# The second down-projection as seven block products, with sums made by accumulating transfers

## The chip, the cores and the metric

The kernel runs on one core of a Trainium2 chip. The metric is the device time in microseconds of one execution, as the median of several runs. TensorE (PE) multiplies, VectorE (DVE) and ScalarE (ACT) work on tiles, GpSimd (POOL) does a little of both and has a DMA queue of its own, and SyncE (SP) issues most of the transfers. Each engine takes its instructions strictly in the order in which they stand in its queue.

## The reference

Two decoder layers over 1024 tokens of 1024 channels, in float32. The first layer mixes by a short convolution and by attention, the second by the RWKV recurrence. Each is followed by the same channel mixer, and the change concerns this one, above all in the second layer:

```python
D_MODEL, SEQ, D_FF = 1024, 1024, 2816

def conv_glu_ffn(x, w_up, conv_w, conv_b, w_down):
    h = causal_dwconv(x @ w_up, conv_w) + conv_b
    gate, up = jnp.split(h, 2, axis=-1)
    return (jax.nn.silu(gate) * up) @ w_down

# in every layer l
x = layer_norm(DN_ALPHA * x + y, ln1_g[l], ln1_b[l])
f = conv_glu_ffn(x, ffn_w_up[l], ffn_conv_w[l], ffn_conv_b[l], ffn_w_down[l])
x = layer_norm(DN_ALPHA * x + f, ln2_g[l], ln2_b[l])
```

## The kernel before

**Products in three parts.** Every float32 operand is split in a rounded part and the rest (`split`, `split_half`: a cast on ScalarE, a subtraction on VectorE), and `mm3` (lines 137 to 139) multiplies high by high, high by low and low by high. A matmul takes 128 rows of the sum and writes 128 x 512.

**The channel mixer** is the generator `ffn(l, ...)`, once for each layer. The 2816 channels are 22 blocks `c` of 128, each with a gate and a value half. The up-projection computes a block by seven products of half-size matrices instead of eight (a Winograd form of Strassen's method). The halves are those of the sum and of the tokens; the sums of weights S1 to S4 (`block`, line 246) are made on VectorE from the raw block `wr`, which SP loads in two tiles per block (line 236), and those of the activations, T1 to T4, once ahead. A product is 12 matmuls, a block 84, some 19 us. Blocks 0 and 1 run as `apart`; the others, 2 to 21, as `chained`, and this part stands in a region with a hand-written order for PE, DVE and ACT (`ORDERED`). SP and POOL are left to the scheduler there. `late(c, i)`, called after product `i` of block `c`, does the convolution of the block before (`tap`), its gate, and with `i` = 7 the product `v` of gate and value, which GpSimd stores to memory as `G[c]` (line 354). It also makes the weight sums of block `c + 1`: with `i` = 1 the sum S1 on VectorE needs the block's second `wr` tile. On VectorE the addition `u` (line 376) stands three instructions behind that sum, and TensorE needs `u` read out before its fourth product. The `wr` loads for this are released by S4 of the block before, at about the end of that block.

**The down-projection** (`down`) follows per half of the tokens: for each of 22 blocks it loads 512 columns of `G[c]` (`gr`) and the weights `wdn[l, c]`, splits both, and adds into eight banks, four token tiles by two halves of the channels. That makes 22 x 8 x 2 x 3 matmuls over both halves. In its last blocks a token tile is finished at a time: the addition to the residual `res`, the statistics, the root on GpSimd (`ln_stats`, line 161), the output steps (lines 496 and 497) and the store. In the second layer it is the end of the program. In the first, the start of the recurrence runs beside it.

```python
            for t in range(4):
                r = rs[t]
                for dh in range(2):
                    for c in range(NC - end, NC):
                        down(c, t, (dh,))
                    nc.vector.tensor_add(r[:, ds_], r[:, ds_], ps[t][dh])
                    tail(4 * tg + t, r, dh)
```

## Time and profile before

| | us |
|---|---|
| median of 3 runs (lowest to highest) | 2764.56 (2763.99 to 2766.55) |
| the profiled execution | 2769.9 |
| its span | 2768.1 |
| PE busy in the span | 2596.0 (94%) |
| DVE, ACT, POOL busy | 1937.0, 1123.2, 275.4 |

The first up-projection runs from about 540 to 970 us, its down-projection to about 1200; the recurrence, with many small operations, takes the time from there to about 2090, the second up-projection that to about 2519, and the second down-projection the rest. TensorE is busy nearly all the time outside the recurrence, so a share of the whole span says little: what a change is worth is read from its stage. Matmuls overlap in their pipeline: a matmul is shown as 0.39 us long, and the next begins 0.23 us after it.

### The profile page before, as it was taken

Reading aid. Unit: us, or ns where it says so; the run is one execution under the profiler, and the core shown is the slowest. Engines: PE = TensorE matmul, PEld = TensorE weight load, DVE = VectorE, ACT = ScalarE, POOL = GpSimd, SP = SyncE. Lnnn points to the kernel's source line nnn. Section 1 sums busy time; section 2 is a strip of 40 time slices with the busy share of each in tenths; the row PEclk is TensorE's granted clock in tenths of the full one; section 3 lists DMA queues with packets and bytes.
Section 4 is the critical chain, followed back from the end, with each engine's and each line's share of the span. In section 5 each row is a group of like instructions: output and inputs, shape, how many; then the busy total and the mean of one; then the engine's idle time right before and its main releaser. Section 6 shows DMA issues by size and latency. Waiting matters only on the chain. (4 is left out here: it accounts for less than half of the span.)

```text
span 2768.1 us, 37639 instructions
## 1 busy us (share of the span) xinstructions
PE 2596.0 (94%) x14736; PEld 2133.1 (77%) x14736; DVE 1937.0 (70%) x3013; ACT 1123.2 (41%) x1706; POOL 275.4 (10%) x247
## 2 busy tenths in 40 slices
PE   8999989989999999999997988688898999999998
PEld 6777778778888888877876766677776888888887
DVE  4655655598888865667778656786758888887673
ACT  3333332344444441426676223333425444444330
POOL 0000000100000003010011011343420000000000
PEclk9999999999999999999998999887999999999999
DMA  5111223212222273633256678786441222225660
GB/s 168 54 46 44 73 88 110 85 61 92 76 84 92 73 264 117 218 128 114 91 183 236 221 219 234 182 195 171 174 147 46 94 82 92 76 84 184 230 217 31
DMA packets 208674, 358.07 MB, mean 129 GB/s; under 512 B 88944, under 2 KB 118256, under 8 KB 208496
## 3 DMA queue, kind: packets, MB, share of 16 engines
q1 hardware_dynamic: 198704, 320.01, 36.5%
q0 software_dynamic: 9792, 35.66, 3.4%
q8 instruction: 116, 1.90, 0.3%
q14 instruction: 62, 0.51, 0.1%
HBM read 255.46 MB, written 95.94 MB: 127 GB/s over the span
## 5 line engine op out<-in xcount | busy, mean ns | idle before, releaser
L137 PE MATMUL up<-x,wu 128*128 128x512 f32 x1232 | 481.8, 393 | 18.5 <-DVE u L312 8.2
L138 PE MATMUL up<-x,wu 128*128 128x512 f32 x1232 | 482.9, 392 | 0.3 <-DVE x L145 0.2
L139 PE MATMUL up<-x,wu 128*128 128x512 f32 x1232 | 482.0, 391 | 0.0
L137 PEld LDWEIGHTS up<-x,wu 128*128 128x128 f32 x1232 | 232.8, 189 | 71.0 <-ACT x L144 14.4
L138 PE MATMUL dn<-wdl,gt 128*128 128x512 f32 x704 | 273.7, 389 | 0.0
L137 PE MATMUL dn<-wdh,gt 128*128 128x512 f32 x704 | 272.2, 389 | 0.3 <-ACT xf L179 0.3
L139 PE MATMUL dn<-wdh,gt 128*128 128x512 f32 x704 | 272.3, 389 | 0.0
L138 PEld LDWEIGHTS up<-x,wu 128*128 128x128 f32 x1232 | 233.1, 189 | 50.7 <-DVE x L145 2.7
L139 PEld LDWEIGHTS up<-x,wu 128*128 128x128 f32 x1232 | 233.0, 189 | 48.7
L254 ACT CAST wu<-ws 128x512 fp32r<-128x512 f32 x176 | 109.3, 623 | 288.4 <-PE up L139 198.8
L137 PE MATMUL pr<-xv,wph 128*128 128x512 f32 x384 | 154.0, 405 | 9.7 <-DVE kp L1156 7.7
L137 PE MATMUL pj<-x,wih 128*128 128x512 f32 x384 | 153.1, 409 | 7.5 <-ACT x L144 7.5
L115 DVE TENSOR_TENSOR wdl<-raw,wdh 128x1024 fp32r<-128x1024 f32 x88 | 109.7, 1246 | 68.7 <-ACT wdh L114 55.5
L138 PE MATMUL pr<-xv,wph 128*128 128x512 f32 x384 | 153.9, 401 | 3.5 <-DVE xv L915 3.5
L139 PE MATMUL pr<-xv,wpl 128*128 128x512 f32 x384 | 154.2, 402 | 2.6 <-DVE wpl L115 2.6
L139 PE MATMUL pj<-x,wil 128*128 128x512 f32 x384 | 153.8, 401 | 0.2 <-DVE wil L115 0.2
L138 PE MATMUL pj<-x,wih 128*128 128x512 f32 x384 | 153.8, 400 | 0.0
L137 PEld LDWEIGHTS dn<-wdh,gt 128*128 128x128 f32 x704 | 132.2, 188 | 27.8 <-ACT xf L179 0.5
L138 PEld LDWEIGHTS dn<-wdl,gt 128*128 128x128 f32 x704 | 132.2, 188 | 27.7 <-DVE wdl L115 0.3
L139 PEld LDWEIGHTS dn<-wdh,gt 128*128 128x128 f32 x704 | 132.2, 188 | 27.3
L114 ACT CAST wdh<-raw 128x1024 fp32r<-128x1024 f32 x88 | 92.6, 1052 | 108.6 <-DMA raw<-wdn 103.5
L254 ACT CAST wu<-wr 128x512 fp32r<-128x512 f32 x132 | 81.4, 623 | 125.1 <-PE up L139 62.8
(319 smaller groups left out, 5230.8 us busy)
## 6 DMA issues: line engine op xcount, KB each, us to landing
wr<-wup SPq DMA_DIRECT2D x88, 512.0 KB, 4.2
raw<-wdn SPq DMA_DIRECT2D x88, 512.0 KB, 4.2
G<-cv POOLq DMA_DIRECT2D x44, 512.0 KB, 2.9
gr<-G SPq DMA_DIRECT2D x88, 256.0 KB, 4.1
bk<-bkS SPq DMA_DIRECT2D x32, 512.0 KB, 5.9
res<-spill SPq DMA_DIRECT2D x24, 512.0 KB, 4.6
raw<-win SPq DMA_DIRECT2D x22, 512.0 KB, 3.7
spill<-res SPq DMA_DIRECT2D x16, 512.0 KB, 2.8
```

Of the source, the lines that this page charges most:

```text
L114: self.nc.scalar.copy(hi, raw)
L115: self.nc.vector.tensor_sub(lo, raw, hi.bitcast(F32))
L137: nc.tensor.matmul(ps, ah, bh, start=first, stop=False, **kw)
L138: nc.tensor.matmul(ps, ah, bl, start=False, stop=False, **kw)
L139: nc.tensor.matmul(ps, al, bh, start=False, stop=last, **kw)
L254: nc.scalar.copy(t[:, lo], src)
```

## The change

The down-projection of the second layer (`fast`) is written anew as `blocks()`. It computes the output's quarters (two halves of tokens, two of channels) by seven products per pair of blocks, 11 pairs, in the order `DOWN` over all pairs: 77 slots of 12 matmuls. Its operands are loaded one slot at a time (`bring`: half a tile of activations, half of weights) and split some slots ahead (`split_slot`). `step`, after every 12 matmuls, hands out the loads, the splits and small VectorE work with a budget. Three products share a group of banks with others, so most sums of products are made in the accumulators, and minus signs are put into operands.

The sums of operands that this needs are made in memory by transfers that GpSimd issues with `accum_op=ALU.add`. Those of the weights (`weight_sums`, T1 to T4 of each pair) are issued in the first layer's up-projection, eight transfers per pair. Those of the activations (`ship`, S1 to S4) are issued in the second's, from the block's value that SP stores in two halves. The store of `G` by GpSimd is gone in the second layer. GpSimd joins `ORDERED`, so its order in the up-projections, and in `blocks()`, is that of the code.

```diff
@@ -29,12 +29,14 @@
-ORDERED = {mybir.EngineType.PE, mybir.EngineType.DVE, mybir.EngineType.Activation}
+ORDERED = {mybir.EngineType.PE, mybir.EngineType.DVE, mybir.EngineType.Activation, mybir.EngineType.Pool}
+DOWN = (1, 6, 2, 5, 3, 7, 4)
+WHEN = (1, 4, 7, 10, 18, 21, 24, 27)
...
-    def ffn(self, l, xo, resid, row, tail, nxt=None):
+    def ffn(self, l, xo, resid, row, tail, nxt=None, out_row=None):
@@ -220,7 +222,43 @@
         lo, hi = slice(0, 512), slice(512, 1024)
-        GS = [self.pd.tile([P, T], F32, name=f"G{l}_{c}") for c in range(NC)]
+        fast = l == 1
+        GS = [] if fast else [self.pd.tile([P, T], F32, name=f"G{l}_{c}") for c in range(NC)]
+        dram = lambda names: [{n: self.pd.tile([P, 512], F32, name=self.nm(n)) for n in names} for _ in range(NC // 2)]
+        SS = dram(("N11", "A12", "N22", "S1", "S2", "S3", "S4")) if fast else []
+        if not fast:
+            self.TS = dram(("T1", "T2", "T3", "T4"))
+
+        def weight_sums(m):
+
+            t = self.TS[m]
+            b = {f"B{i}{j}": wdn[l + 1, 2 * m + i - 1, :, j * 512 - 512:j * 512] for i in (1, 2) for j in (1, 2)}
+            put = nc.gpsimd.dma_start
+            for n, x in (("T1", "B11"), ("T3", "B12"), ("T2", "B11"), ("T4", "B21")):
+                put(t[n], b[x])
+            for n, x in (("T1", b["B12"]), ("T3", b["B22"]), ("T2", t["T3"]), ("T4", t["T2"])):
+                put(t[n], x, accum_op=ALU.add, max_dma_last_dim=512)
+
+        def store(c, g, v):
+
+            if not fast:
+                nc.vector.tensor_tensor(v, g, v, op=ALU.mult)
+                nc.gpsimd.dma_start(GS[c], v)
+                return
+            for h in (lo, hi):
+                if (h is hi) == (c % 2 == 1):
+                    nc.vector.scalar_tensor_tensor(v[:, h], g[:, h], -1.0, v[:, h], ALU.mult, ALU.mult)
+                else:
+                    nc.vector.tensor_tensor(v[:, h], g[:, h], v[:, h], op=ALU.mult)
+
+        def ship(c, v):
+
+            s, put = SS[c // 2], nc.gpsimd.dma_start
+            for n, h in zip(("N11", "S1") if c % 2 == 0 else ("A12", "N22"), (lo, hi)):
+                nc.sync.dma_start(s[n], v[:, h])
+            for n, x, add in (("S3", "S1", 0), ("S3", "N11", 1)) if c % 2 == 0 else (("S1", "N22", 1), ("S2", "N22", 0), ("S4", "A12", 0), ("S2", "S3", 1), ("S4", "S2", 1)):
+                put(s[n], s[x], **({"accum_op": ALU.add, "max_dma_last_dim": 512} if add else {}))
+
         W = [{} for _ in range(NC)]
         sums = {"S1": ("A21", "A22", ALU.add), "S2": ("S1", "A11", ALU.subtract),
                 "S3": ("A11", "A21", ALU.subtract), "S4": ("A12", "S2", ALU.subtract)}
@@ -294,8 +332,9 @@
         def value(c):
             w = W[c]
             v = conv(w["h"], NC + c)
-            nc.vector.tensor_tensor(v, w["g"], v, op=ALU.mult)
-            nc.gpsimd.dma_start(GS[c], v)
+            store(c, w["g"], v)
+            if fast:
+                ship(c, v)
             w.clear()
 
         def apart(c, i):
@@ -350,8 +389,11 @@
                 elif i == 5:
                     tap(w["v"], w["h"], NC + b, 2)
                 elif i == 7:
-                    nc.vector.tensor_tensor(w["v"], w["g"], w["v"], op=ALU.mult)
-                    nc.gpsimd.dma_start(GS[b], w["v"])
+                    store(b, w["g"], w["v"])
+                    if not fast:
+                        w.clear()
+                elif i == 3 and fast:
+                    ship(b, w["v"])
                     w.clear()
             name = {1: "S1", 2: "S2", 3: "S3", 4: "S4"}.get(i)
             if name and c + 1 < NC:
@@ -384,6 +426,165 @@
             if i == 4:
                 add(w["h"][:, lo], w["u"][:, hi], ps)
 
+
+
+        terms = {1: ("N11", "B11"), 6: ("S2", "T2"), 2: ("A12", "B21"), 5: ("S1", "T1"), 3: ("S4", "B22"), 7: ("S3", "T3"), 4: ("N22", "T4")}
+        slots = [(i, m) for i in DOWN for m in range(NC // 2)]
+        raws, parts = {}, {}
+
+        def bring(k):
+            i, m = slots[k]
+            a, b = terms[i]
+            t = raws[k] = self.W("dr", F32)
+            nc.sync.dma_start(t[:, lo], SS[m][a])
+            nc.sync.dma_start(t[:, hi], self.TS[m][b] if b[0] == "T" else wdn[l, 2 * m + int(b[1]) - 1, :, int(b[2]) * 512 - 512:int(b[2]) * 512])
+
+        def split_slot(k):
+            t = raws.pop(k)
+            h, w = self.U("dh", F32R), self.U("dl", F32R)
+            parts[k] = h, w
+            if slots[k][0] in (2, 6):
+                nc.scalar.activation(h[:, lo], t[:, lo], AF.Copy, scale=-1.0)
+                nc.scalar.copy(h[:, hi], t[:, hi])
+                nc.vector.scalar_tensor_tensor(w[:, lo], t[:, lo], -1.0, h[:, lo].bitcast(F32), ALU.mult, ALU.subtract)
+                nc.vector.tensor_sub(w[:, hi], t[:, hi], h[:, hi].bitcast(F32))
+            else:
+                self.split(t, h, w)
+
+        def blocks():
...
+            def later(f, *a, cost=0.7, front=False, after=0):
+                work.insert(0, (f, a, cost, after)) if front else work.append((f, a, cost, after))
...
+            def out(t, v):
+                (mv, rstd), r = stats[t], rs[t]
+                nc.vector.scalar_tensor_tensor(r[:, v], r[:, v], mv[:, 0:1], fin[0][:, v], ALU.subtract, ALU.mult)
+                nc.vector.scalar_tensor_tensor(r[:, v], r[:, v], rstd, fin[1][:, v], ALU.mult, ALU.add)
+                nc.sync.dma_start(self.out[t * P:t * P + P, v], r[:, v])
...
+            def finished(i, t):
+
+                a, b = rs[t], rs[4 + t]
+                if i == 1:
+                    nc.scalar.copy(at(us, t), X[t])
+                elif i == 6:
+                    later(put, at(u2, t), at(us, t), Y[t], front=True)
...
+                elif i == 5:
+                    put(b[:, hi], b[:, hi], Y[t])
+                    later(put, b[:, hi], b[:, hi], at(us, t))
+                    later(put, b[:, lo], b[:, lo], at(u2, t), ALU.subtract)
...
+                elif i == 7:
+                    put(b[:, hi], b[:, hi], Z[t])
+                    later(halves, 4 + t, 1)
+                elif i == 4:
+                    put(b[:, lo], b[:, lo], Z[t], ALU.subtract)
+                    halves(4 + t, 0)
+                    norm(4 + t)
+                    for v in (lo, hi):
+                        later(out, 4 + t, v, cost=1.4, after=1)
+
+            for i in (1, 6, 2, 5, 7, 3):
+                later(late, NC, i, cost=1.4)
+            tick, mms, ready = [0], [0], [4, 2]
...
+            def step():
+
+                n = tick[0]
+                tick[0] += 1
+                ahead = 5 if n < 55 else 7
+                for _ in range(2):
+                    if ready[1] < min(len(slots), n + 1 + ahead):
+                        if ready[0] <= ready[1]:
+                            bring(ready[0])
+                            ready[0] += 1
+                        split_slot(ready[1])
+                        ready[1] += 1
+                    if n % 2:
+                        break
+                while ready[0] < min(len(slots), ready[1] + 3):
+                    bring(ready[0])
+                    ready[0] += 1
+                if n in WHEN:
...
+                left = 1.3
+                while work and left > 0:
+                    f, a, cost, after = work.pop(0)
+                    if after:
...
+                    f(*a)
+                    left -= cost
+            for p, i in enumerate(DOWN):
+                if i == 1:
+                    X[:] = [x[:, h] for x in (self.A("dn"), self.A("dn")) for h in (lo, hi)]
+                if i == 6:
+                    Y[:] = [self.B("dn") for _ in range(4)]
+                if i == 7:
+                    Z[:] = [x[:, h] for x in (self.A("dn"), self.A("dn")) for h in (lo, hi)]
+                ps = X if i in (1, 2) else Z if i in (7, 4) else Y
+                n = NC // 2
+                first = 3 if i in (3, 4) else 1
+                last = 5 if i == 4 else 3 if i in (5, 7) else 1
+                groups = [range(first)] + [range(m, m + 1) for m in range(first, n - last)] + [range(n - last, n)]
+                for g in groups:
+                    for k in g:
+                        assert p * n + k in parts, (i, k, ready)
+                    for t in range(4):
+                        for m in g:
+                            h, w = parts[p * n + m]
+                            tk = slice(t * P, t * P + P)
+                            self.mm3(ps[t], h[:, tk], w[:, tk], h[:, hi], w[:, hi], m == 0 and i in (1, 6, 7), m == n - 1, skip_group_check=True)
+                            mms[0] += 3
+                            if mms[0] % 12 == 0:
+                                step()
+                        if g[-1] == n - 1:
+                            finished(i, t)
+            while work:
+                f, a, cost, after = work.pop(0)
+                f(*a)
+
         seq = [(c, i) for i in FIRST for c in range(2)]
         seq += [(c, i) for c in range(2, NC) for i in (1, 6, 2, 5, 7, 3, 4)]
         for c in range(2):
@@ -409,10 +610,21 @@
                     apart(c, i)
                 else:
                     chained(n, c, i)
-                if n == len(seq) - 3:
+                if n > 14 and i == 3 and not fast:
+                    for m in (0, 1) if c == 3 else (c // 2,) if c % 2 else ():
+                        weight_sums(m)
+                if fast:
+                    if n >= len(seq) - 4:
+                        bring(n - len(seq) + 4)
+                    if n >= len(seq) - 2:
+                        split_slot(n - len(seq) + 2)
+                elif n == len(seq) - 3:
                     operands(0, 0)
                     operands(0, 1)
                 yield
+            if fast:
+                blocks()
+                return
             for i in (1, 6, 2, 5, 7):
                 late(NC, i)
         for tg in range(2):
@@ -1578,7 +1790,7 @@
         def mixed(i, l, w, resid, alpha, out_args, last_tail, nxt=None):
 
             tail, res = k.make_tail(f"l{i}g", f"l{i}b", None, "hl")
-            gen = k.ffn(l, res["xo"], res["spill"], row(i), last_tail, nxt)
+            gen = k.ffn(l, res["xo"], res["spill"], row(i), last_tail, nxt, row(3))
             res["fill"] = lambda n: drain(gen, n)
 
             def after(get):
```

On GpSimd's queue in the first up-projection, before (`G_n` is the stored value of block n):

```order
L354 DMA G_4_4023<-cv_4983 128x1024
L354 DMA G_5_4024<-cv_5122 128x1024
L354 DMA G_6_4025<-cv_5261 128x1024
```

and after (`T` are the weight sums; 128x512 rows are copies, 128x4x128 and 512x128 accumulate):

```order
L246 DMA G_4_4023<-cv_5043 128x1024
L238 DMA T_735_4049<-wdn 128x512
L238 DMA T_737_4051<-wdn 128x512
L238 DMA T_736_4050<-wdn 128x512
L238 DMA T_738_4052<-wdn 128x512
L240 DMA T_735_4049<-wdn 128x4x128
L240 DMA T_737_4051<-wdn 128x4x128
L240 DMA T_736_4050<-T_737_4051 512x128
L240 DMA T_738_4052<-T_736_4050 512x128
L246 DMA G_5_4024<-cv_5190 128x1024
L246 DMA G_6_4025<-cv_5329 128x1024
```

Between two stores of values there now stand eight transfers, after every second store.

On GpSimd's queue in the second up-projection, after, one pair of blocks (before there are two stores of `G` like those above in its place):

```order
L260 DMA S_2634_17001<-S_2632_16999 16x4096
L260 DMA S_2634_17001<-N_2629_16996 512x128
L260 DMA S_2632_16999<-N_2631_16998 512x128
L260 DMA S_2633_17000<-N_2631_16998 16x4096
L260 DMA S_2635_17002<-A_2630_16997 16x4096
L260 DMA S_2633_17000<-S_2634_17001 512x128
L260 DMA S_2635_17002<-S_2633_17000 512x128
```

Two of the seven belong to the even block, five to the odd one; 16x4096 are copies, 512x128 accumulate.

On SP's queue in the same stage, before:

```order
L236 DMA wr_18504<-wup 128x1024
L236 DMA wr_18367<-wup 128x1024
L236 DMA wr_18643<-wup 128x1024
L236 DMA wr_18506<-wup 128x1024
L236 DMA wr_18782<-wup 128x1024
```

and after:

```order
L258 DMA N_2629_16996<-cv_18015 128x512
L258 DMA S_2632_16999<-cv_18015 128x512
L274 DMA wr_18307<-wup 128x1024
L274 DMA wr_18163<-wup 128x1024
L258 DMA A_2630_16997<-cv_18158 128x512
L258 DMA N_2631_16998<-cv_18158 128x512
L274 DMA wr_18450<-wup 128x1024
L274 DMA wr_18309<-wup 128x1024
```

Two stores of a value's halves now stand ahead of each pair of weight loads.

At the end of the program on VectorE, before, the last token tile:

```order
L471 TENSOR_TENSOR res_21604<-res_21604,dn_21147 128x512
L489 BN_STATS bst_21827<-res_21604 128x6
L158 BN_AGGR mv_21849<-bst_21827 128x2
L160 TENSOR_SCALAR rstd_21851<-mv_21849 128x1
L496 SCALAR_TENSOR_TENSOR res_21604<-res_21604,mv_21849,bc_20853 128x512 x2
L497 SCALAR_TENSOR_TENSOR res_21604<-res_21604,rstd_21851,bc_20855 128x512 x2
```

and after, from the last token tile's addition on:

```order
L468 TENSOR_TENSOR res_21119<-res_21119,dn_21669 128x512
L481 BN_STATS bst_21988<-res_21119 128x6
L160 BN_AGGR mv_22141<-bst_21988 128x2
L162 TENSOR_SCALAR rstd_22143<-mv_22141 128x1
L488 SCALAR_TENSOR_TENSOR res_21052<-res_21052,mv_22113,bc_20459 128x512
L489 SCALAR_TENSOR_TENSOR res_21052<-res_21052,rstd_22115,bc_20461 128x512
L488 SCALAR_TENSOR_TENSOR res_21052<-res_21052,mv_22113,bc_20459 128x512
L489 SCALAR_TENSOR_TENSOR res_21052<-res_21052,rstd_22115,bc_20461 128x512
L488 SCALAR_TENSOR_TENSOR res_21119<-res_21119,mv_22141,bc_20459 128x512
L489 SCALAR_TENSOR_TENSOR res_21119<-res_21119,rstd_22143,bc_20461 128x512
L488 SCALAR_TENSOR_TENSOR res_21119<-res_21119,mv_22141,bc_20459 128x512
L489 SCALAR_TENSOR_TENSOR res_21119<-res_21119,rstd_22143,bc_20461 128x512
```

The output steps of the tile before (`res_21052`) now stand behind the last tile's norm.

## Rows read from the trace of the kernel before

**Rows 1.** Windows: busy time and instructions of each engine, granted clock, DMA share, GB/s

```profile
core 0: us, PE busy (x) PEld busy (x) DVE busy (x) ACT busy (x) POOL busy (x), PEclk, DMA share, GB/s
600.00:1000.00 400.00, 400.00 (x1766) 331.25 (x1765) 325.04 (x426) 185.13 (x248) 14.08 (x24) 1.00 0.27 97
2200.00:2400.00 200.00, 199.06 (x878) 164.22 (x877) 166.26 (x221) 91.75 (x126) 5.33 (x10) 1.00 0.22 79
...
2520.00:2720.00 200.00, 200.00 (x885) 165.64 (x884) 122.95 (x146) 69.26 (x87) 6.47 (x7) 1.00 0.61 206
```

**Rows 2.** Groups, 2516 to 2769 us: tiles, shapes, count, busy us, mean ns, idle before

```profile
L115 DVE TENSOR_TENSOR wdl<-raw,wdh 128x1024 fp32r<-128x1024 f32 x44 | 53.8, 1223 | 36.6 <-ACT wdh L114 28.7 <-issue 3.6 <-PE dn L138 2.9
...
L145 DVE TENSOR_TENSOR gt<-gr,gt 128x512 fp32r<-128x512 f32 x43 | 29.4, 685 | 7.6 <-ACT gt L144 7.5
...
L497 DVE SCALAR_TENSOR_TENSOR res<-res,rstd,bc 128x512 f32<-128x512 f32 x16 | 11.4, 745 | 0.0
...
L452 DVE TENSOR_TENSOR res<-res,bc 128x1024 f32<-128x1024 f32 x8 | 9.8, 1221 | 7.0 <-DMA res<-spill 7.0
```

**Rows 3.** Timeline of VectorE at the end: start us, us, instruction [idle before]

```profile
2758.72 0.69 DVE L471 TENSOR_TENSOR res<-res,dn 128x512 f32<-128x512 f32 x1 [2.33 <-PE dn L139]
2759.44 0.69 DVE L489 BATCH_NORM_STATS2 bst<-res 128x6 f32<-128x512 f32 x1
2760.17 0.21 DVE L158 BATCH_NORM_AGGREGATE mv<-bst 128x2 f32<-128x12 f32 x1
...
2760.49 1.40 DVE L496 SCALAR_TENSOR_TENSOR res<-res,mv,bc 128x512 f32<-128x512 f32 x2
2761.81 1.41 DVE L497 SCALAR_TENSOR_TENSOR res<-res,rstd,bc 128x512 f32<-128x512 f32 x2
```

**Rows 4.** Waits, 600:965, then 2155:2515: total us, times, longest

```profile
DVE ws L246 <- DMA wr<-wup: 29.4, 18, 2.1
...
DVE ws L246 <- DMA wr<-wup: 32.5, 18, 3.3
...
PE up L137 <- DVE u L376: 0.9, 2, 0.8
```

**Rows 5.** Timeline of VectorE in the second up-projection, three places

```profile
2256.42 0.69 DVE L246 TENSOR_TENSOR ws<-wr 128x512 f32<-128x512 f32 x1 [2.66 <-DMA wr<-wup]
...
2371.73 0.69 DVE L246 TENSOR_TENSOR ws<-wr 128x512 f32<-128x512 f32 x1 [3.27 <-DMA wr<-wup]
...
2372.95 1.28 DVE L273 SCALAR_TENSOR_TENSOR cv<-gi,par,cv 128x1022 f32<-128x1022 f32 x1
...
2390.13 0.69 DVE L246 TENSOR_TENSOR ws<-wr 128x512 f32<-128x512 f32 x1 [1.56 <-DMA wr<-wup]
```

**Rows 6.** Timeline of TensorE behind the second of them

```profile
2373.71 0.39 PE L139 MATMUL up<-x,wu 128*128 128x512 f32 x1
2374.87 0.50 PE L137 MATMUL up<-x,wu 128*128 128x512 f32 x1 [0.78 <-DVE u L376]
```

**Rows 7.** DMA, 2364:2373, then 2384:2392: packets, MB, share; KB, us to landing

```profile
q8 instruction: 1, 0.02, 0.6%
...
wr<-wup SPq DMA_DIRECT2D x2, 512.0 KB, 5.0
...
wr<-wup SPq DMA_DIRECT2D x2, 512.0 KB, 4.0
```

**Rows 8.** Timeline of GpSimd and of SP's queue around 2385 us

```profile
2381.64 0.53 POOL L354 DMA_DIRECT2D G<-cv  x1 [20.01 <-DVE cv L353]
...
2385.32 0.80 SPq L236 DMA_DIRECT2D wr<-wup  x2
```

**Rows 9.** The page's DMA issues: count, KB each, median us to landing

```profile
G<-cv POOLq DMA_DIRECT2D x44, 512.0 KB, 2.9
...
out<-res SPq DMA_DIRECT2D x16, 256.0 KB, 2.5
```

**Rows 10.** DMA issues, 980:994

```profile
bc<-lng SPq DMA_DIRECT2D x1, 512.0 KB, 6.6
...
G<-cv POOLq DMA_DIRECT2D x1, 512.0 KB, 9.6
```

39 lines of the change are left out of this document (added).

## The prediction

> **What bounds the kernel now.** I read the windows view first, because one share for the whole span hides the stages. [...] 1766 matmuls in 400 us and 885 in 200 us are one every 0.226 us. In these stages the time is the count of 512-column matmuls times 0.226 us, and every one taken out shortens the program by that much as long as the other engines keep ahead. VectorE is the one that could fail to: 325 of 400 us in the first up-projection, 166 of 200 in the second, 123 of 200 in the second down-projection [rows 1].
>
> The second thing to see is how little slack the up-projections have beside TensorE. The waits view shows VectorE waiting 18 times in each of them for the weight block `wr` of the next channel block: 29.4 us in all in the first, at most 2.1, and 32.5 us in the second, at most 3.3; TensorE waited for VectorE's `u` there only twice, 0.9 us in all [rows 4]. The timeline has three of these waits side by side: 1.56 us is the ordinary one, 2.66 and 3.27 are late ones [rows 5]. Behind the last stands the only sizeable hole: the next matmul starts 1.16 us after its forerunner instead of 0.226, so 0.93 us late, released by `u` [rows 6]. A wait longer by 3.27 - 1.56 = 1.71 us thus cost 0.93, and 0.78 of it was free. Past that, a late `wr` delays TensorE one for one. This matters because the change puts new transfers where these loads run.
>
> **Matmuls removed.** Before: 22 channel blocks x 8 token tiles x 2 halves x 3 = 1056. After: 7 products x 11 pairs x 4 token tiles x 3 = 924. 132 fewer at 0.226 us: **-29.8 us**, 238.7 to 208.8 us for the stage. This holds if no engine falls behind, so the others come next.
>
> **VectorE in the second down-projection.** After has 77 slots to split, 55 with one 1024-wide subtraction (1.223 us) and 22 with two 512-wide ones (0.685 and, for the one that also changes sign, 0.745): 67.3 + 31.5 us [rows 2]. The residuals take 16 x 1.22 = 19.5, some 52 additions and statistics of 512 columns at 0.69 take 35.9, the 32 output steps at 0.745 take 23.8, norms and the last block's taps about 9.4 [rows 2, 5]. In all 187 us of 208.8, or 90%, where it was 61% [rows 1]. It stays under TensorE and five to seven slots ahead (a slot is 12 matmuls, 2.7 us), so I put it at 0. Its cover is thin: from about 11% more it would be the bound.
>
> **Loads of that stage.** 77 slots x 0.5 MB, the residuals and four broadcast rows are about 47 MB in 209 us, 223 GB/s. Before moved 206 GB/s at a DMA share of 0.61 [rows 1], so the share goes to about 0.66. The broadcast rows are slow ones (6.6 us for 512 KB under load, [rows 10]), and four of them stand together at the start; slots are loaded some eight ahead, 20 us, and I put this at 0, at most 3. S2 of the last pair is summed only after block 21's values are there; its chain of stores and sums is about 15 us, and its matmuls come some 57 us into the stage: 0.
>
> **Tail.** Before, after the last matmul at 2758.7 VectorE runs 4.5 us (addition, statistics, norm, four output steps), to 2763.2 [rows 3], and one token tile's last matmuls take 36 x 0.226 = 8.1 us, so nothing is left over of the tile ahead. After, the last group has five pairs per tile: 15 matmuls, 3.4 us from tile to tile, while VectorE has about 4.65 us for each: 0.72 + 0.73 + 0.4 up to the norm, and four steps of 0.70 [rows 3]. From 10.2 us before the end 4 x 4.65 + 0.5 for the first root on GpSimd gives 19.1, so VectorE ends 8.9 us after the last matmul, not 4.5: **+4.4 us**. The order of the rows on VectorE shows it: two tiles' output steps stand behind the last matmuls, not one's.
>
> **The second up-projection.** The product is now stored in two halves (0.745 + 0.685 against 1.22, 0.2 us on an engine with that much to spare), and its store moves from GpSimd's queue to SP's. SP stands in order, but these two stores are ready 3 to 4 us before the `wr` loads that stand behind them (GpSimd's store of a value began at 2381.64, the next `wr` loads at 2385.32, [rows 8]), so SP does not delay `wr`. The sums do collide with it. The halves land 2.5 us after issue [rows 9], at about 2384.2 in that block; GpSimd then issues a memory-to-memory transfer at 0.53 us each [rows 8], so the first packets run from about 2385, where `wr` runs from 2385.3 to 2389.7. For an even block this is one copy ahead of the bulk of `wr`, and an accumulating transfer behind it: 0. For an odd block an accumulating transfer and two copies go out together. Those copies are cut in 16 rows of 16 KB, one for each of the 16 engines. No row shows an accumulating transfer. The nearest row is one 16 KB packet on one engine: the instruction queue brought one while the late `wr` was under way, 0.6% of 16 engines' 9 us, 0.86 us; the two loads then landed after 5.0 us in the median instead of 4.0, and VectorE waited the 1.71 us more [rows 5, 7]. So the bounds per odd block are 0 (the packets pass before or behind) and 2 x 1.71 - 0.78 = 2.6 us; the row itself gives 0.93, and as there are two copies and a sum I take 1.1. Nine odd blocks (3 to 19) have a `wr` load to disturb: **+9.9 us**, between 0 and 23.
>
> [...] GpSimd's store of the first down-projection, issued after SP's loads, landed after 9.6 us instead of 2.9 [rows 9, 10]: it stood behind what had been issued before. [...]
>
> **The first up-projection.** 88 transfers of 256 KB join GpSimd's queue in eleven sets of eight, four copies and four sums, mostly one set after each second store. The store of the next value stands behind the set and its waits; it is read only in the down-projection, more than 20 us later, and GpSimd has nothing else to do there (14 of 400 us busy, [rows 1]). So the pinned order costs nothing: 0. The copies start right behind the store, in rows of 2 KB, and 1.5 MB at the store's pace (512 KB in about 1.5 us of packets within its 2.9 us) is through at about the time `wr` starts; the first sums then run beside it in short packets. Same bounds, 0 to 2.6; I take 0.35 for nine blocks: **+3.2 us**.
>
> **Moves elsewhere.** Between the layers, in the recurrence, the orders differ in a few dozen rows of TensorE's small matmuls and of the others, and nothing is added there. I put it at 0, +-3.
>
> **Sum.** -29.8 + 4.4 + 9.9 + 3.2 = -12.3 us. The profiled execution took 2769.9 (span 2768.1, 1.8 around it) and would give 2757.6. The median of the runs is 5.3 lower, 2764.56, and the forecast is **2752**.
>
> **Rivals.**
> 1. The sums slip past the loads, and the collision terms are 0: 2764.6 - 29.8 + 4.4 = **2739**. For it: 0.78 us of each wait is free, and the two `wr` loads fill the engines for only some 3 us of each 19 us block. Against: the times above put the odd blocks' copies right on them.
> 2. **Slower: the sums delay nearly every `wr` load.** If an accumulating transfer of 256 KB in short packets takes some 5 us of the engines, a set or chain reaches into the next block's load too, and all 36 waits of [rows 4] grow. At 0.93 each, as in [rows 6], that is 33.5 us, less 25.4: **2773**. It decides from 31 / 36 = 0.86 us per wait. For it: GpSimd's store under load took 9.6 us [rows 10]. Against: sums come in pairs of blocks, so half of the waits have little beside them.
> 3. The gain is eaten, not overtaken: collisions of 20 to 31 us, or VectorE at 90% falling behind in the second down-projection: **2760 to 2770**, no measurable change. The change would then do what it says to TensorE's count, and TensorE would wait for what it saved.
>
> **How the numbers follow.** This kernel's measurement tells 0.2% (5.5 us) from no change. The forecast, 2744 to 2759, gets 0.42; rival 1 (2735 to 2744) 0.25; rival 3 gets 0.17; rival 2 0.16. So faster 0.67, same 0.17, slower 0.16. The range of 8 in 10 reaches from rival 1's lower side to rival 2's time: 2736 to 2774.
>
> **What would show it.** The matmul count of the second down-projection is 924 at 0.226 us with no holes; VectorE is near 90% there and ends about 9 us after the last matmul. In the second up-projection VectorE's wait for `wr` alternates, about 1.6 us behind even blocks and about 3.4 behind odd ones, and TensorE has nine holes of about 1 us released by `u`; in the first there are shorter ones. If the waits stay at 1.6 everywhere, rival 1 holds; if all grow, rival 2. I am wrong in kind if TensorE waits in the second down-projection for a split slot, or if the time moves between the layers.

## The result, and the profile of the changed kernel

The changed kernel takes 2805.68 us (median of 4 runs, 2801.23 to 2814.55), the kernel before 2765.45 beside it: a ratio of 1.0148, 95% interval 1.0128 to 1.0168. It is 40 us slower, where 2752 was forecast and 2736 to 2774 given as the range. The sign was that of rival 2, the price higher still.

The two profiled executions differ by 33.0 us in span: the one before lies some 4 us above the median beside it, the one after 3 us below its own. The table cuts each span at the start of an up-projection's first matmul, at the end of its last one, and at the start of a down-projection's last one; the last four columns are experiments that come below.

| stage, us | before | after | e1 | e3 | e4 | e8 |
|---|---|---|---|---|---|---|
| ahead of the first up-projection | 533.1 | 530.5 | 533.1 | 532.3 | 534.0 | 533.6 |
| first up-projection | 438.3 | 461.4 | 437.9 | 437.5 | 462.6 | 438.1 |
| first down-projection | 243.3 | 243.3 | 243.3 | 243.3 | 243.4 | 243.3 |
| between the layers | 866.2 | 868.0 | 864.8 | 865.8 | 876.9 | 861.7 |
| second up-projection | 439.4 | 462.3 | 437.0 | 466.8 | 437.4 | 437.0 |
| second down-projection | 238.1 | 223.3 | 217.9 | 220.1 | 217.4 | 210.3 |
| from the last matmul's start | 9.8 | 12.4 | 11.9 | 12.0 | 11.9 | 9.9 |
| span | 2768.1 | 2801.1 | 2745.9 | 2777.9 | 2783.7 | 2733.7 |

So each up-projection lost 23 us, and the second down-projection won 14.8 of the 29.8 us that its missing matmuls are worth. The part between the layers, which none of these kernels edits, moves by up to 11 us all the same. It takes 8.9 us more in e4 than in the changed kernel, though VectorE, ScalarE and GpSimd have the same instructions in the same order there. So a difference of the whole program of a few us is not read as an edit's effect here; that of its stage is.

The windows of the changed kernel, the first two at the same times as [rows 1], the third in its second down-projection (columns as there):

```profile
core 0: us, PE busy (x) PEld busy (x) DVE busy (x) ACT busy (x) POOL busy (x), PEclk, DMA share, GB/s
600.00:1000.00 400.00, 382.65 (x1661) 312.97 (x1660) 309.14 (x408) 175.15 (x236) 83.17 (x105) 0.99 0.56 139
2200.00:2400.00 200.00, 189.77 (x822) 154.41 (x821) 155.28 (x216) 85.41 (x118) 27.59 (x34) 0.99 0.48 122
2570.00:2770.00 200.00, 193.73 (x830) 158.36 (x829) 149.31 (x185) 81.28 (x99) 10.78 (x11) 0.97 0.71 237
```

Where [rows 1] has 1766 matmuls in 400 us there are now 1661, and VectorE does less in the same time, too: both wait for something else. The DMA share doubled, from 0.27 to 0.56 and from 0.22 to 0.48. The waits view names it (total us, times, longest; first up-projection, then the second, then the second down-projection):

```profile
DVE ws L284 <- DMA wr<-wup: 55.6, 18, 5.8
...
PE up L139 <- DVE u L418: 17.4, 10, 3.3
...
DVE ws L284 <- DMA wr<-wup: 61.2, 17, 4.9
...
PE up L139 <- DVE u L418: 19.9, 11, 2.5
...
PE dn L139 <- DVE res L468: 5.3, 4, 2.6
PE dn L139 <- ACT u L496: 2.6, 2, 1.9
```

VectorE's waits for `wr` were 29.4 and 32.5 us in [rows 4], and TensorE's for `u` 0.9. One such wait in VectorE's timeline (start us, us, [idle before <- releaser]), and TensorE behind it:

```profile
2405.11 1.28 DVE L311 SCALAR_TENSOR_TENSOR cv<-gi,par,cv 128x1023 f32<-128x1023 f32 x1
2410.47 0.69 DVE L284 TENSOR_TENSOR ws<-wr 128x512 f32<-128x512 f32 x1 [4.08 <-DMA wr<-wup]
...
2412.88 0.68 DVE L418 TENSOR_TENSOR u<-u,up 128x512 f32<-128x512 f32 x1
```

```profile
2411.64 0.39 PE L141 MATMUL up<-x,wu 128*128 128x512 f32 x1
2413.61 0.50 PE L139 MATMUL up<-x,wu 128*128 128x512 f32 x1 [1.58 <-DVE u L418]
```

The block sum S1 waits 4.08 us where 1.56 is ordinary [rows 5]; `u` stands behind it on VectorE, and the next matmul starts 1.97 us after its forerunner, 1.74 late: 4.08 - 1.56 - 0.78 = 1.74. In this block the slack of 0.78 us read from [rows 5, 6] holds to the hundredth. The late blocks are every second one, as forecast: in the second up-projection the odd blocks 3 to 19 wait 4.1 to 5.0 us and cost 1.9 to 4.0 each (21.9 in all); of the even ones two are late as well (10 and 14, which is the one shown), and the others wait 2.1 to 2.6 and cost next to nothing. In the first it is the blocks behind a set of weight sums (4, 6, 8, ...) that cost 1.5 to 5.2 each, and block 5 with 1.1.

The dearest holes cost more than their wait, because TensorE's clock falls behind them. The windows of the longest one (in the first up-projection: the matmul starts 3.4 us late) and right behind it, and the one at the border of products 1 and 6:

```profile
673.00:677.00 4.00, 1.32 (x6) 0.75 (x4) 2.55 (x4) 0.00 (x0) 0.00 (x0) 1.00 0.87 119
677.00:681.00 4.00, 3.41 (x10) 2.70 (x11) 4.00 (x6) 2.04 (x3) 1.04 (x1) 0.68 0.45 54
...
2593.00:2603.00 10.00, 7.44 (x21) 5.20 (x20) 9.97 (x15) 7.42 (x14) 2.06 (x3) 0.69 1.05 341
```

The granted clock is 1.00 in the window in which TensorE waits and 0.68 in the one behind it, where it is 0.50 from 678.5 to 681 us; behind the border it is 0.50 from 2597 to 2603 us.

### The profile page after: what moved, and what is told of

The parts are those of the page before. It is cut to its first block, busy times and chain, and to the rows that moved or that the text cites. A ratio compares the mean times of both kernels' runs of the same rounds, so it can differ in the third digit from the quotient of the medians.

```text
span 2801.1 us, 37843 instructions
## 1 busy us (share of the span) xinstructions
PE 2564.3 (92%) x14604; PEld 2095.1 (75%) x14604; DVE 1964.8 (70%) x3066; ACT 1136.0 (41%) x1721; POOL 403.6 (14%) x390
## 3 DMA queue, kind: packets, MB, share of 16 engines
q0 software_dynamic: 57664, 67.38, 11.5%
## 5 line engine op out<-in xcount | busy, mean ns | idle before, releaser
L140 PEld LDWEIGHTS up<-x,wu 128*128 128x128 f32 x1232 | 234.0, 190 | 50.5 <-DVE x L147 2.7
L140 PE MATMUL dn<-wdl,gt 128*128 128x512 f32 x352 | 137.0, 390 | 0.0
L139 PE MATMUL dn<-wdh,gt 128*128 128x512 f32 x352 | 136.3, 390 | 0.3 <-ACT xf L181 0.3
L141 PE MATMUL dn<-wdh,gt 128*128 128x512 f32 x352 | 136.2, 389 | 0.0
L139 PE MATMUL dn<-dh 128*128 128x512 f32 x308 | 122.5, 398 | 7.8 <-DVE res L468 5.3
L299 DVE TENSOR_TENSOR wu<-ws,wu 128x512 fp32r<-128x512 f32 x176 | 120.3, 684 | 4.0 <-ACT wu L292 4.0
L140 PE MATMUL dn<-dl,dh 128*128 128x512 f32 x308 | 121.6, 395 | 0.0
L141 PE MATMUL dn<-dh,dl 128*128 128x512 f32 x308 | 121.6, 395 | 0.0
L311 DVE SCALAR_TENSOR_TENSOR cv<-hv,par,cv 128x1023 f32<-128x1023 f32 (+1 forms) x88 | 112.3, 1276 | 0.1
```

The source lines that it names most:

```text
L139: nc.tensor.matmul(ps, ah, bh, start=first, stop=False, **kw)
L140: nc.tensor.matmul(ps, ah, bl, start=False, stop=False, **kw)
L141: nc.tensor.matmul(ps, al, bh, start=False, stop=last, **kw)
L299: nc.vector.tensor_sub(t[:, hi], src, t[:, lo].bitcast(F32))
L311: nc.vector.scalar_tensor_tensor(cc[:, k:], src[:, :T - k], self.pc_(wname, 88 - 44 * k + ct), cc[:, k:], ALU.mult, ALU.add)
```

## The experiments

Theory: the memory-to-memory sums run beside the `wr` loads, these land late, VectorE waits in order, `u` is late. Rivals: GpSimd's pinned order or its longer queue, SP's new stores, or a cost that does not pass through `wr` at all. The pinned order by itself needs no run: with GpSimd pinned and nothing else changed, the kernel before has the same instructions in the same order on every queue.

### e1 and e2: the load that VectorE waits for, issued earlier

SP issues the `wr` loads of a block in pairs. The half that S1 reads (part 1) stood behind the other half of the block after it, which waits for a raw buffer. Exchanging their homes frees it:

```diff
-                    t = self.U("wr") if part else self.RAW("wr")
+                    t = self.RAW("wr") if part else self.U("wr")
```

> The changed kernel, with the homes of the two wr loads exchanged: the half that S1 reads first (part 1) goes to the ring of two raw buffers, which come free after the cast of product 4, and part 0 to the big ring. So the load that VectorE waits for is issued earlier by most of a block; nothing else is changed. Theory (late loads): the transfers of sums make the wr loads land late, VectorE waits for them in order, and TensorE waits for u; with the load early both up-projections go back from 461.0 and 461.9 us to 438 to 442 each, the second down-projection stays at 222 to 226, and the kernel comes to 2757 to 2768. Rival (the sums cost by another way than the wait for wr: VectorE or ScalarE slower beside GpSimd, TensorE's operands late for other reasons): the waits for wr go and the up-projections stay above 455 each, 2790 to 2806.

Measured: 2747.95 us, ratio to before 0.9924 (0.9898 to 0.9949). VectorE's waits for `wr` are gone from both up-projections, TensorE's for `u` too, and the stages are back at 437.9 and 437.0 us. The theory holds: all that the two stages lost passes through this one wait. No transfer was taken out. The time is below what was expected, since the second down-projection gained another 5 us (it had been costed at 222 to 226) and the part between the layers 3.

The same line in the kernel before:

> The kernel before, with the same exchange of the two wr loads. Theory: there VectorE's wait for wr (1.56 us in most blocks) did not reach TensorE, 0.78 us more would have been free, so the waits go and the time stays, 2760 to 2769. Rival: TensorE's rate in the up-projections hangs on these waits also before; then some 10 us or more are won, below 2756.

Measured: 2765.95 us, ratio 0.9987 (0.9972 to 1.0001): no difference that shows. In the kernel before the waits for `wr` were slack, as the prediction had it, and the exchange is no gain of its own. It is worth something only beside the sums.

### e3 and e4: one set of sums taken out

e3 leaves out the weight sums of the first up-projection (e3's down-projection loads plain blocks of `wdn` instead), e4 GpSimd's sums of the second, with SP's stores kept (e4's down-projection loads stored halves in place of S2, S3 and S4):

```diff
                     for m in (0, 1) if c == 3 else (c // 2,) if c % 2 else ():
-                        weight_sums(m)
+                        pass
```

```diff
-            for n, x, add in (("S3", "S1", 0), ("S3", "N11", 1)) if c % 2 == 0 else (...):
-                put(s[n], s[x], **({"accum_op": ALU.add, "max_dma_last_dim": 512} if add else {}))
```

> The changed kernel without the sums of the weights: GpSimd's transfers in the first up-projection are left out, and the second down-projection loads four blocks of wdn in their place, so the output is another one. Theory (late loads): the first up-projection goes back from 461.0 to 437 to 441 us, the second stays at 460 to 463, the kernel comes to 2778 to 2786. Rival (the pinned order, the extra instructions or their waits on GpSimd's queue, not the transfers' traffic): the G stores still stand in the pinned order, so the first up-projection stays above 455.

> The changed kernel without GpSimd's sums of the stored halves in the second up-projection; SyncE's two stores for each block stay, and the down-projection loads N11, A12 and N22 in place of S3, S4 and S2, so the output is another one. Theory (late loads by the memory-to-memory transfers): the second up-projection goes back from 461.9 to 439 to 444 us, the first stays at 460 to 463, the kernel comes to 2780 to 2787. Rival (SyncE's stores, which stand in front of the wr loads on one queue and wait for v): the second up-projection stays above 455.

Measured: e3 2775.42 us (ratio 1.0028, 1.0009 to 1.0046), first up-projection 437.5; e4 2786.09 (1.0061, 1.0043 to 1.0078), second up-projection 437.4. Each set of sums costs its own stage, and the other stage stays late. (e3's time is below the 2778 to 2786 expected, and its second up-projection, 466.8 us, above the 460 to 463.) VectorE's waits, e3 in the first up-projection and e4 in the second:

```profile
DVE ws L284 <- DMA wr<-wup: 29.0, 18, 1.8
```

```profile
DVE ws L282 <- DMA wr<-wup: 30.4, 17, 2.9
```

These are the 29.4 and 32.5 of [rows 4] again. SP's stores are cleared: they are all there in e4. GpSimd's G stores are all there in e3, in their pinned order.

### e5 and e10: copies alone, accumulating transfers alone

e5 drops the accumulating half of the weight sums. e10 puts the copies on SP's queue, where they move to the program's start, so that the first up-projection carries the accumulating half alone (written at the later place that e6 has below).

```diff
-            for n, x in (("T1", b["B12"]), ("T3", b["B22"]), ("T2", t["T3"]), ("T4", t["T2"])):
-                put(t[n], x, accum_op=ALU.add, max_dma_last_dim=512)
```

```diff
-                put(t[n], b[x])
+                nc.sync.dma_start(t[n], b[x])
```

> The changed kernel (wr loads as they were) with the weight sums' plain copies alone: the four accumulating transfers of each pair are left out, so T1 to T4 hold single blocks and the output is another one. Half of the transfers' bytes are gone. Theory (the wr loads share the DMA engines with whatever else moves then, byte by byte): the four copies start together just ahead of the wr loads and stand beside them most, so more than half of the first up-projection's 23 us stays: 449 to 457 us there. Rival (accumulating transfers are what delays the loads, by their many small packets): the first up-projection falls to 438 to 442.

> The changed kernel (wr loads as they were) with the weight sums' 44 plain copies on SyncE's queue, which the scheduler puts at the program's start among the first loads; the accumulating transfers stay on GpSimd's queue in the first up-projection (in the place of e6). So the first up-projection carries the accumulating half alone. Theory (bytes beside the loads): with the copies gone the sums start right behind the G store, some 6 us ahead of the wr loads, and take part of the copies' place: 440 to 452 us there, less than with the copies alone (456.5). Rival (accumulating transfers delay the loads by their number of packets): 455 or more. The copies' 11.5 MB at the start delay the first loads: the part ahead of the first up-projection grows from 533 us by 10 to 40.

Measured, in a single run each: e5 2796.62 us, first up-projection 456.5; e10 2823.41 us, 454.7, with 28 us more ahead of it. So copies alone cost 18 us, accumulating transfers alone 16, both together 23 (22 to 24 in the three kernels that have both, the changed kernel, e4 and e6). e5 came as the theory had it; e10's stage lies above the theory's 440 to 452 and just under the rival's 455. In most blocks either kind delays the loads nearly as long as both: from block 8 on, S1 behind a set waits 3.1 to 4.4 us in e5, 3.0 to 4.0 in e10 and 3.7 to 4.9 in the changed kernel.

The DMA view shows it: packets, MB and share of the 16 engines by queue, and the loads' time to landing. GpSimd's transfers are on q0, the loads on q1. First the changed kernel, 748.5 to 755 us, at a late block, then 768.9 to 775, at the next block, which is on time:

```profile
q0 software_dynamic: 561, 0.90, 56.5%
q1 hardware_dynamic: 286, 1.04, 49.1%
...
wr<-wup SPq DMA_DIRECT2D x2, 512.0 KB, 6.2
...
q1 hardware_dynamic: 288, 1.05, 50.5%
q0 software_dynamic: 86, 0.28, 11.3%
...
wr<-wup SPq DMA_DIRECT2D x2, 512.0 KB, 4.0
```

Then e10, 777.5 to 784 us, with accumulating transfers ahead of the loads:

```profile
wr<-wup SPq DMA_DIRECT2D x2, 512.0 KB, 5.9
```

Over the whole window of the late block each queue has about half of the engines' time, but they do not share it evenly from moment to moment. The same view for one microsecond each, from 1.0 to 2.0 us behind the first load's issue: the late block (749.63 to 750.63), the one on time (770.2 to 771.2; q0 has 0.1%), the late one of e10 (778.76 to 779.76, q0 alone) and, in the second up-projection, an odd block (2383.07 to 2384.07, q0 alone). A share can be over 100%: a packet's whole time is counted where it starts, and in the last of these windows 313 packets, the longest of 0.74 us, come to 132.0%, so some of them overlap.

```profile
q0 software_dynamic: 70, 0.23, 102.2%
q1 hardware_dynamic: 3, 0.01, 7.4%
...
q1 hardware_dynamic: 39, 0.16, 62.7%
...
q0 software_dynamic: 248, 0.13, 114.7%
...
q0 software_dynamic: 313, 0.17, 132.0%
```

When the loads should begin, GpSimd's earlier transfers have all of the engines, whether they are copies or sums, and the loads start only as these end. It is so at all nine late blocks behind a set in the first up-projection and at six of the nine odd blocks in the second. In the late block above the four copies were issued from 744.89 to 747.0 us and the loads at 748.63; from 751.63 to 753.63 the loads then have 88.0% of the engines and q0 2.2%, and from 754 the two sums that GpSimd issued from 749.25 on stand on the loads' last packets (q0 128.3%, q1 10.3% up to 755.6). So the changed kernel has copies ahead of the loads and sums at their end. In the three other odd blocks the sums run between the two loads, and there are stretches with both queues side by side; 2468.3 to 2470.5 us:

```profile
q0 software_dynamic: 144, 0.46, 65.2%
q1 hardware_dynamic: 105, 0.41, 48.1%
```

Either way the loads, which need 3.1 us of all engines (50.5% of 6.1 us in the window that is on time), land some 2 us later.

### e6 and e9: the same transfers at another moment

e6 issues a pair's weight sums one block later, after product 6. e9 also puts a small wait ahead: GpSimd first reads a column of the next block's S1, the very sum that waits for `wr`.

```diff
-                if n > 14 and i == 3 and not fast:
-                    for m in (0, 1) if c == 3 else (c // 2,) if c % 2 else ():
+                if n > 14 and not fast and (i == 6 and c % 2 == 0 and c > 2 or i == 3 and c == NC - 1):
+                    for m in (0, 1) if c == 4 else ((c - 1) // 2,):
```

```diff
+                if n > 14 and not fast and (i == 1 and c % 2 == 0 and c > 2 or i == 3 and c == NC - 1):
+                    if i == 1:
+                        nc.gpsimd.tensor_copy(self.S(1, "gate"), W[c + 1]["S1"][:, 0:1])
+                    for m in (c // 2 - 2,) if i == 1 else (9, 10):
```

> The changed kernel (wr loads as they were) with the weight sums issued at another moment: after product 6 of the even block that follows, when its wr loads have landed, instead of after product 3 of the odd block, just ahead of them. All transfers and all results stay. Theory (a collision in time): the four copies and most of the sums are through before the next wr loads start, and the first up-projection falls from 461 to 438 to 446 us. Rival (the transfers' amount costs, whenever they run, or GpSimd's queue does): it stays above 455. The G store stands behind these transfers on GpSimd's queue and becomes some 10 us later, with no reader near. Second up-projection and down-projection stay at 462 and 222 to 226.

Measured, in a single run: 2806.5 us, first up-projection 460.0: nothing moved. GpSimd's timeline says why, first in the changed kernel, then in e6:

```profile
744.35 0.55 POOL L246 DMA_DIRECT2D G<-cv  x1 [17.86 <-DVE cv L245]
744.89 2.10 POOL L238 DMA_DIRECT2D T<-wdn  x4
```

```profile
747.53 0.55 POOL L246 DMA_DIRECT2D G<-cv  x1 [17.81 <-DVE cv L245]
748.07 2.10 POOL L238 DMA_DIRECT2D T<-wdn  x4
```

The copies wait for nothing, so they go out 0.54 us after the G store ahead of them, wherever in the block they are written. An order on a queue is not a time. e6 says nothing for or against the theory, since it did not do what it was for.

> The changed kernel (wr loads as they were); in the first up-projection GpSimd copies one column of S1 of the next block ahead of each pair's weight sums, in the even blocks. S1 is the sum that waits for wr, so the transfers can't start before the wr loads have landed; they then have some 17 us until the next. All transfers and results stay (the last two pairs go behind block 21). e6 moved them in GpSimd's order alone, and they started at the same moment as before, right behind the same G store (744.89 against 748.07 us), since no wait holds them there. Theory (a collision in time): the first up-projection falls from 461 to 438 to 445 us. Rival (the amount of traffic costs, whenever it runs): it stays above 455. Second up-projection and down-projection as in the changed kernel, 460 to 467 and 219 to 224.

Measured, in a single run: 2797.97 us, first up-projection 448.8. It lies between the two expectations: half of the loss is gone. GpSimd's timeline in e9, and the next block's loads on SP's queue:

```profile
753.50 0.51 POOL L615 COPY gate<-ws 128x1 f32<-128x1 f32 x1 [8.85 <-DVE ws L284]
753.96 2.10 POOL L238 DMA_DIRECT2D T<-wdn  x4
...
770.20 1.00 POOL L240 DMA_DIRECT2D T<-T  x1 [4.12 <-DMA T<-T]
770.84 0.93 POOL L246 DMA_DIRECT2D G<-cv  x1
...
766.81 0.80 SPq L274 DMA_DIRECT2D wr<-wup  x2
```

The even blocks, late in the changed kernel, now cost 0; the odd ones, which cost next to nothing there, cost 0.3 to 2.1 from block 5 on, because the chain of four sums, one after the other, is still running at 770.20 when the next `wr` loads have been issued at 766.8. That the late blocks change places with the moment is what the theory asks for; that such a set, whose sums wait for one another and take some 22 us here from the first copy's issue to the last landing, does not fit between loads 19 us apart was missed in the expectation. The second up-projection took 472.0 us here, 462 to 467 in the other kernels that leave it as in the changed one; why it varies was not followed up.

### e7 and e8: the second down-projection

With the loads early, e1 still had six holes in the second down-projection, 0.8 to 2.8 us each and 7.6 in all. TensorE's waits there in e1, and two of them in the timelines of TensorE and VectorE:

```profile
PE dn L139 <- DVE res L468: 5.3, 4, 2.6
PE dn L139 <- ACT u L496: 1.4, 2, 0.7
```

```profile
2691.53 0.39 PE L141 MATMUL dn<-dh,dl 128*128 128x512 f32 x1
2693.01 0.50 PE L139 MATMUL dn<-dh 128*128 128x512 f32 x1 [1.09 <-DVE res L468]
...
2697.00 0.39 PE L141 MATMUL dn<-dh,dl 128*128 128x512 f32 x1
2700.02 0.50 PE L139 MATMUL dn<-dh 128*128 128x512 f32 x1 [2.64 <-DVE res L468]
```

```profile
2692.28 0.68 DVE L468 TENSOR_TENSOR res<-res,dn 128x512 f32<-128x512 f32 x1
...
2699.29 0.68 DVE L468 TENSOR_TENSOR res<-res,dn 128x512 f32<-128x512 f32 x1
```

The holes always come in twos, and in products 1, 7 and 4 alone: those whose four sums lie in two tiles of two banks and are read as soon as each is finished (product 2 sums in the tiles of product 1, but `step` hands its reads out later). VectorE (or ScalarE) reads one half of a tile, and the matmuls of the other half wait for it. e7 gives these products four tiles of one bank, and the two-bank tiles to products 6, 5 and 3, with the reads after product 5 issued by pairs; e8 also lengthens the last group. Both stand on e1's exchange.

```diff
-                    X[:] = [x[:, h] for x in (self.A("dn"), self.A("dn")) for h in (lo, hi)]
+                    X[:] = [self.B("dn") for _ in range(4)]
...
-                    Y[:] = [self.B("dn") for _ in range(4)]
+                    Y[:] = [x[:, h] for x in (self.A("dn"), self.A("dn")) for h in (lo, hi)]
...
-                    Z[:] = [x[:, h] for x in (self.A("dn"), self.A("dn")) for h in (lo, hi)]
+                    Z[:] = [self.B("dn") for _ in range(4)]
...
-                            finished(i, t)
+                            for v in (() if t % 2 == 0 else (t - 1, t)) if i == 5 else (t,):
+                                finished(i, v)
```

```diff
-                last = 5 if i == 4 else 3 if i in (5, 7) else 1
+                last = 7 if i == 4 else 3 if i in (5, 7) else 1
```

> The wr loads exchanged as in e1, and the accumulators of the second down-projection exchanged too: products 1 and 2 and products 7 and 4 sum in four tiles of one bank each, products 6, 5 and 3 in two tiles of two banks; the reads after product 5 are issued by pairs. Theory of the holes: TensorE waited for the reading of one half of a two-bank tile before it wrote the other half (0.84, 0.85, 1.25, 2.80, 0.94, 0.94 us in e1, and 1.9 us at the lower clock after them), so all of these go, the second down-projection falls from 217.9 to 209 to 211 us and the kernel, with VectorE's end no earlier than its own work allows, comes to 2738 to 2745 against e1's 2748. Rival (VectorE is simply behind there, since it is busy 94% from 2676 to 2696 us): the same waits come back at products 7 and 4, dn stays at 215 to 218, no gain on e1.

> e7 with the last group of product 4 made of seven slots instead of five, so that the last four row blocks end 4.8 us apart instead of 3.4, and VectorE's 4.7 us for each fit in between. Theory: the tail after the last matmul falls from 11.9 to 8 to 9 us, 3 us less than e7, if the slots are split in time; rival: the splits of the last slots come late by as much, TensorE waits in product 4 and nothing is won.

Measured: e7 2736.28 us, ratio to before 0.9892 (0.9875 to 0.9909), second down-projection 209.8 us. The time is 2 us below the 2738 to 2745 expected. All six holes are gone, and one wait is left:

```profile
PE dn L140 <- DVE dl L117: 0.5, 1, 0.5
```

The rival that VectorE is simply behind there falls: with the same work the waits at products 7 and 4 are gone, and some 10 us after product 7 it waits for TensorE itself (12.1 us in e1, 7.1 in e7). e8: 2734.27 us, ratio 0.9874 (0.9853 to 0.9894). From the last matmul's start to the end it takes 9.9 us against e7's 12.9: the 3 us less that were expected, though not the 8 to 9 us; 0.5 of it came back in the stage ahead, and the difference of the whole program is within the intervals. Its VectorE, at the end, and its last matmul:

```profile
2725.21 0.68 DVE L468 TENSOR_TENSOR res<-res,dn 128x512 f32<-128x512 f32 x1
...
2729.60 0.75 DVE L489 SCALAR_TENSOR_TENSOR res<-res,rstd,bc 128x512 f32<-128x512 f32 x1
```

```profile
2723.86 0.39 PE L141 MATMUL dn<-dh,dl 128*128 128x512 f32 x1
```

The last row block is taken up 1.35 us after the last matmul's start, right behind the output steps of the block before, and none of those is left for later. e8 is 1.3% faster than the kernel before, and by the two ratios (0.9874 and 1.0148) 2.7% faster than the changed kernel, with all of the change in it.

## Why the prediction was wrong, point by point

- **Matmuls removed, -29.8 us: right in size.** Where next to nothing waits (e7) the stage takes 209.8 us against 208.8 forecast and 238.1 before.
- **Second up-projection, +9.9 us: mechanism right, term mis-sized; it measured +22.9.** The path (sums, `wr`, VectorE in order, `u`), the odd blocks, and the free 0.78 us were right. The step that failed is the price of an odd block: I took two 16 KB packets as all that stands in the loads' way and forecast a wait of 3.4 us. The nine odd blocks waited 4.5 us on average and cost 2.4 each instead of 1.1, since the sum in short packets, for which I had no row, was ahead of the loads too and had the engines when they should have begun (132.0% at 2383.07 us). The bound of 23 us, from a wait twice as long, was the time that came, in part by luck: two even blocks, forecast at 0, gave 2.9 of it.
- **First up-projection, +3.2 us: mis-sized; it measured +23.1.** The step was "1.5 MB at the store's pace is through at about the time `wr` starts". It is not: the copies still held all of the engines (102.2%) in the microsecond in which the loads should have begun, and when they are taken away (e10) the sums do the same (114.7%).
- **How queues share.** The row (GpSimd's store behind the loads issued before it, [rows 10]) was near what came at 15 of the 18 late blocks that were forecast: what had been issued earlier went first there, and the loads waited for it (102.2% against 7.4% from 749.63 us). It is not the whole, since stretches with both queues side by side are there as well (65.2% and 48.1% from 2468.3 us); what decides between the two was not shown. My error was to let the load give way to two pieces of 16 KB, where one queue kept all of the engines for a microsecond and more.
- **VectorE in the second down-projection, 0, and its loads, 0 to 3: wrong; 14.5 us were lost.** The busy share was no bad guide to VectorE's capacity (75% measured in the window, 90% forecast), but I read only the share. What each product's matmuls wait for, the tile that their accumulator shares with another row block, stood in the code and was not followed; the prediction called a wait of TensorE for a split slot there "wrong in kind", and the waits came, only for an accumulator's readers. In the changed kernel, and not in e1, the first of these waits met a late load: ScalarE's read of X stood behind a cast that waited 2.38 us for `dr<-S`, which made the hole at 2593 us and the lower clock behind it (0.69 from 2593 to 2603 us). The six holes of the changed kernel take 8.9 us, and 5.1 more went to the lower clock behind two of them, at 2593 and at 2753 us (0.50 from 2754 to 2756); in e1 nearly the same holes (7.6 us) had next to no such stretch behind them.
- **Tail, +4.4 us: it measured +2.6.** The last matmul of the changed kernel and VectorE's last instruction:

```profile
2788.71 0.39 PE L141 MATMUL dn<-dh,dl 128*128 128x512 f32 x1
```

```profile
2796.41 0.75 DVE L489 SCALAR_TENSOR_TENSOR res<-res,rstd,bc 128x512 f32<-128x512 f32 x1
```

  VectorE ends 8.4 us after that matmul's start; before it was 4.9 (the last matmul started at 2758.3, VectorE ended at 2763.2, [rows 3]). That is 3.5 us more; what follows, up to the landing of the last store, was 0.9 us shorter than before, which the sum had as equal.
- **Pinned order, SP's stores and the moves elsewhere, 0:** right (e3, e4; -2.6 ahead, +1.8 between the layers).
- **The rivals.** Rival 2 had the right sign and place, and too little chance; it put 0.93 us on 36 waits, 33.5 in all, where 21 late ones at 2.3 came to some 48. None of the cases put the collisions of both up-projections near their upper bound at once, 23 + 23 us, though the row of 9.6 us for one store [rows 10] said what a loaded set of engines does. A range that takes in the bounds of the unknown costs, as it should, would have reached some 2785 (2764.6 - 25.4 + 46), still short of the measured time, since VectorE's part in the second down-projection stood at 0.

## What to carry to other kernels

Transfers that no engine waited for cost 23 us in each up-projection here, since they had the DMA engines (102.2% at 749.63 us, 132.0% at 2383.07) when a load that is waited for should have begun: count the engines' time of what was issued just ahead, in the few microseconds where they meet, and not over the stage. Before adding traffic, look at which load is waited for in order and whether its issue can be made earlier; here one exchanged pair of buffers turned a loss of 1.5% into a gain of 0.8% (e1). And a place in a queue's order set no time where nothing there waited (in e6 the copies still went out 0.54 us after the G store), and two accumulators in one tile were, in this kernel, one accumulator to every wait (six holes, 7.6 us in e1, gone in e7).

## What the runs showed of the hardware that was not expected

- In one microsecond a memory-to-memory sum in 512-byte packets moved 0.13 MB (e10 from 778.76 us, 114.7% of the engines' time), copies 0.23 MB (the changed kernel from 749.63 us, 102.2%) and 0.41 MB (from 748.63 us, 101.5%): a byte of the sum took 2.0 to 3.6 times the engines' time.
- Loading moved to where nothing seemed to use it was not free: 11.5 MB of copies at the program's start (e10) put off the first up-projection by 28 us, 561.6 against 533.1.
- One hole of 3.4 us in a stage that otherwise keeps TensorE busy was followed by a stretch at a granted clock of 0.68, so that it cost 5.2 us in all. The hole of 2.8 us in product 7 was followed by the lower level in the changed kernel (0.86 from 2752 to 2764 us) and not in e1 (1.00 from 2699 to 2711).
